# Queries and keys of a two-layer encoder made by rows of 512 columns and turned by VectorE and DRAM, in place of products by channels

## The chip, the cores and the metric

The kernel runs on one core of one Trainium2 chip, as one launch. The metric is the device time of the launch in microseconds (us), the median of the runs; smaller is better. Profiles are of one execution each, taken by the hardware profiler.

## What is computed

Two layers, each with a token mixer and a gated MLP, on 256 tokens of 1024 channels, all in float32. The mixer, cut to what matters here:

```python
u, q, k, v, g_pool, g_attn = split(rmsnorm(h) @ w_in)     # 1024, 1536, 1536, 1536, 1024, 1024 columns
pool_out = per_group(centred_mean(u) - u) @ w_pool * pool_scale
logits = q @ k.T * HEAD_DIM**-0.5 + bias                  # 12 heads of 128 channels, 3 groups of 4 heads
p = softmax over a head of all three groups together      # keys +-64 strides of 1, 4, 16 tokens
attn = p @ v
merged = sigmoid(g_pool) * (pool_out @ w_a) + sigmoid(g_attn) * (attn @ w_b)
h = h + merged @ w_o
```

The MLP (`w_up`, a convolution over three tokens, gelu, `w_down`) follows, and a last norm after the second layer.

## The kernel before

**Products.** A float32 weight is loaded raw (1 MB a load, on SP's queue), and cut into *pieces* of 128 x 1024 elements. ScalarE rounds a piece to the high part `wh` (L201), VectorE subtracts to get the low part `wl` (L203); this is called the split. The activation is kept as two parts too, and a product is three matmuls: high by high, high by low, low by high. Raw loads have 3 buffers, split pieces 5 (`RAW`, `BUFS`, L104), and `W.get()` (L224) asks for splits of up to three pieces ahead (`LOOK`). All splits go through ScalarE and VectorE in the order of the program's list of pieces.

There are two ways to form a product with the normed activation `x2`. *By channels* (`proj` L551, `two_sums` L530): a piece is 128 output channels; for each of 8 parts of the depth one matmul of `wh` against 512 columns (both parts of 256 tokens) and one of `wl` against 256, 16 matmuls a piece; the result has channels on partitions. *By tokens* (`by_tokens` L672, `v_sum` L661): the tokens are on the output's partitions, a piece is 256 rows of depth by 512 output columns, 12 matmuls of 512 columns; four pieces make 512 columns, in two PSUM tiles, one for each half of the tokens.

**Order in a layer.** Values (by tokens), the pooling branch's `u` (by channels), then queries and keys: `PAIRS` (L38) lists six pairs of heads, and for each, two pieces of queries and two of keys go through `proj` (L1115 to L1147). Then `po2 @ w_a` (`pa`, two blocks by tokens, L1151), the first gate (two blocks, L1163), the second gate with `attn @ w_b` (L1177), `w_o`, and the MLP. The w_pool product (`pool_out`, L993) is dealt out over the second pair.

**Queries and keys.** Four heads (group 0) are kept in two parts, `qh`, `kh` and `qkl` (ScalarE L1131, VectorE L1132 and L1136); the other eight are kept as plain float32 `q`, `kk` (ScalarE L1142, VectorE L1143). The factor HEAD_DIM^-0.5 is put on the queries here.

**Attention.** `scores(hh)` (L1025) makes, for each half of the tokens, a PSUM tile `s_ps`: three matmuls of the high and low parts (L1029), and a float32 one for each of the other groups (L1034, two records each). VectorE adds the bias (L1040) and takes the maximum (L1045), ScalarE the exponential (L1048), VectorE the reciprocal of the sum (L1050) and the scaling (L1051). `start_turn` hands the two tiles to `cross` (L704): VectorE transposes 32 x 32 blocks (L711), SP writes them to DRAM (L713), waits, and reads them back with 4 DMAs in another order (L718), which completes a transposition. `turn` splits part of it (L1072, L1073), `weigh` (L1076) multiplies by the values into `o_ps`, and ScalarE and VectorE keep that as `at2` (L1091, L1092). The MLP uses the same `cross` for its gate.

**What sets the order.** The table `steps` (L1095) says after which piece of the stages from the fourth pair on each of these is written into the program; `step()` runs it. From the program a scheduler makes one fixed list of instructions for each engine. An engine works through its list in order, so an instruction that waits holds up what is behind it. SP's list holds the loads and the crossings together; `loads_behind` puts named loads behind named reads.

Of the kernel before, what the change touches and what calls it, by code (L numbers as in the profile page):

```python
# [16 lines left out]
P = 128  # L17
D = 1024
# [19 lines left out]
PAIRS = (2, 4, 0, 1, 3, 5)  # L38
# [58 lines left out]
class Weights:  # L97
# [8 lines left out]
    def __init__(self, tc, pool, idle):  # L106
        self.tc, self.nc, self.pool, self.idle = tc, tc.nc, pool, idle
        self.loads, self.pieces = [], []
        self.n_loaded, self.n_split, self.n_got = 0, 0, 0
        self.raw, self.split = {}, {}  # L110
        self.live = set()
        self.behind, self.later = (), []
        self.last = [None, None]
        self.loads_behind = {}
# [12 lines left out]
    def load(self, upto):  # L127
        while self.n_loaded < min(upto, len(self.loads)):
            src, shape, tag = self.loads[self.n_loaded]
            name = f"raw{self.n_loaded}"  # L130
            if tag is None:
                t = self.pool.tile([P, *shape], F32, tag="raw", bufs=self.RAW, name=name)
            else:
                t = self.idle.tile([P, *shape], F32, tag=tag, name=name)
            held = self.loads_behind.get(self.n_loaded)
            with self.tc.issue_after(held.ins) if held else ExitStack():
                self.last_load = self.nc.sync.dma_start(out=t, in_=src)
            self.raw[self.n_loaded] = t
            self.n_loaded += 1

# [101 lines left out]
def encoder(ctx, tc, x, w_in, w_pool, pool_scale, w_a, w_b, w_o, norm1, norm2, w_up, conv_w,  # L242
# [28 lines left out]

    first_up = []
    for l in range(DEPTH):
# [10 lines left out]
        for n, c in enumerate(PAIRS):  # L284
            pool = ([], [])
            if n == 1:
                pool = W.add(
                    w_pool[l].rearrange("g (k p) c -> p (g k) c", p=P), (8, 256),
                    [((lambda t, j=j: t[:, 4 * j : 4 * j + 4, :]), (4, 256)) for j in range(2)],
                )  # L290
                pool = (pool[:1], pool[1:])
            W.use(pool[0] + cols(w_in[l], C_Q + c * 256))
            W.use(pool[1] + cols(w_in[l], C_K + c * 256))
# [378 lines left out]
    def by_tokens(x2, n, at_once=1, then=None, ps=None, begin=0, end=None):  # L672
# [4 lines left out]
        for i0 in range(begin, n if end is None else end, at_once):  # L677
            held = [W.get() for _ in range(at_once)]
# [25 lines left out]
    def cross(rows, y, z, name, but=1, after=None):  # L704
# [4 lines left out]
        with tc.issue_after(after.ins) if after else ExitStack():  # L709
# [3 lines left out]
        nc.sync.dma_start(  # L713
            out=d.rearrange("(t p) q x -> p t (q x)", t=2),
            in_=y.rearrange("p t q c j -> p t (q c j)"),
        )
# [5 lines left out]
        W.loads_behind[W.n_loaded + but] = there  # L722
# [180 lines left out]
    for l in range(DEPTH):  # L903
# [114 lines left out]
        qh = big.tile([P, HPG, 2, P], F32R, tag="q0", name="qh")  # L1018
        kh = big.tile([P, HPG, 2, P], F32R, tag="k0", name="kh")
        q = big.tile([P, NH - HPG, 2, P], F32, tag="q1", name="q")  # L1020
        kk = big.tile([P, NH - HPG, 2, P], F32, tag="k1", name="k")
        at2 = big.tile([P, HPG, 2, 2, P], F32R, tag="at2", name="at2")
        probs, ptiles = {}, {}

        def scores(hh):  # L1025
            for t in range(2):
                ps = acc.tile([P, 512], F32, tag="acc", name="s_ps")
                for m, (a, b) in enumerate(((qh, kh), (qh, kl), (ql, kh))):
                    nc.tensor.matmul(  # L1029
                        ps[:, 0:256], a[:, hh, t, :], b[:, hh].rearrange("p t m -> p (t m)"),  # L1030
                        start=(m == 0), stop=(m == 2),
                    )
                for g in (1, 2):
                    nc.tensor.matmul(  # L1034
                        ps[:, 128 + g * 128 : 256 + g * 128], q[:, (g - 1) * HPG + hh, t, :],
                        kk[:, (g - 1) * HPG + hh, t, :],
                        start=True, stop=True,
                    )
                s = sm.tile([P, 512], F32, tag="s", name="s")
                nc.vector.tensor_add(  # L1040
                    out=s.rearrange("p (a b) -> p a b", a=2), in0=ps.rearrange("p (a b) -> p a b", a=2),
                    in1=bias_of(t, hh),
# [15 lines left out]
        turned_p = big.tile([P, 2, 2 * 4, 4, 32], F32, tag="ybig", name="turned_p")  # L1058

        def start_turn(hh):  # L1060
            y = sm.tile([P, 2, 4, 4, 32], F32, tag="gain", bufs=1, name="turning")
            there = cross([probs[hh, t] for t in range(2)], y, turned_p[:, hh % 2], "turning")
# [3 lines left out]
        def turn(hh):  # L1066

            z = turned_p[:, hh % 2]
# [7 lines left out]
        def weigh(hh):  # L1076
# [31 lines left out]
        places = iter(range(20))  # L1108
# [5 lines left out]

        for m, c in enumerate(PAIRS):  # L1115
            if m == 1:
                po2 = two_parts("m2", "po2")
                pool_parts = pool_out(po2)
            if m == 2:

                qkl = big.tile([P, 2, HPG, 2, P], F32R, tag="xn", name="qkl")
                ql, kl = qkl[:, 0], qkl[:, 1]
            for n in range(4):
                if m == 1:
                    next(pool_parts)
                src, rest = (halves(a) for a in proj(x2, 1 + (m != 1)))
                hd = 2 * c + n % 2
                scale = HD**-0.5 if n < 2 else 1.0
                if hd < HPG:
                    hi, lo = ((qh, ql) if n < 2 else (kh, kl))  # L1130
                    nc.scalar.mul(out=hi[:, hd], in_=src, mul=scale)  # L1131
                    nc.vector.scalar_tensor_tensor(  # L1132
                        out=lo[:, hd], in0=src, scalar=scale, in1=hi[:, hd].bitcast(F32),
                        op0=ALU.mult, op1=ALU.subtract,
                    )
                    nc.vector.scalar_tensor_tensor(  # L1136
                        out=lo[:, hd], in0=rest, scalar=scale, in1=lo[:, hd].bitcast(F32),
                        op0=ALU.mult, op1=ALU.add,
                    )
                else:  # L1140
                    o = (q if n < 2 else kk)[:, hd - HPG]
                    nc.scalar.mul(out=o, in_=rest, mul=scale)  # L1142
                    nc.vector.scalar_tensor_tensor(  # L1143
                        out=o, in0=src, scalar=scale, in1=o, op0=ALU.mult, op1=ALU.add
                    )
                if m >= 3 and n % 2:
                    step()  # L1147


        pa = big.tile([P, 2, D], F32, tag="xn", name="pa")  # L1150
        for cc in HALVES:  # L1151
            ps = by_tokens(po2, 4, then=step)
            for t in range(2):
                nc.scalar.copy(out=pa[:, t, cc], in_=ps[t])

        def gate():
            ps = by_tokens(x2, 4, then=step if steps else None)
            th = big.tile([P, 2, 512], F32, tag="gates", name="gates")
# [4 lines left out]
        for cc in HALVES:  # L1163
# [211 lines left out]
```

## Time and profile before

| | |
|---|---|
| median of 3 runs | 859.91 us (859.57 to 860.25) |
| the profiled execution | 859.81 us, of which the profile's span is 858.0 us |
| VectorE busy | 661.2 us, 77% of the span |
| ScalarE busy | 493.8 us, 58% |
| GpSimd busy | 32.0 us, 4% |
| DMA | 186.81 MB, 217 GB/s over the span, 63.8% of 16 engines' time |

PE is TensorE, DVE VectorE, ACT ScalarE, POOL GpSimd, SP SyncE (its queue issues nearly all DMAs). Busy time is the union of an engine's instructions. In groups, "x24 | 5.7, 708" means 24 instructions, 5.7 us busy in all, 708 ns for one; matmuls overlap in the pipeline, so their own duration is longer than the time from one start to the next.

### The profile page before, as it was taken

How to read it: one execution, taken by the hardware profiler on the slowest of the kernel's cores; microseconds unless marked ns; L12 is line 12 of the kernel's file. 1: busy time of each engine (PE TensorE's matmuls, PEld its weight loads, DVE VectorE, ACT ScalarE, POOL GpSimd, SP SyncE). 2: the span in 40 equal slices, each digit the busy share in tenths (PEclk: the TensorE clock that was granted, in tenths of full speed). 3: DMA queues.
4: the chain of work that ended last, by engine and by line, in shares of the span. 5: the costliest groups of instructions: out<-in, count | busy, mean ns of one | idle time of the engine just before them, and what ended most of it. 6: DMA issues, size and time to landing. Idle time of an engine off the chain costs nothing.

```text
span 858.0 us, 11823 instructions
## 1 busy us (share of the span) xinstructions
PE 851.6 (99%) x4343; PEld 727.9 (85%) x4343; DVE 661.2 (77%) x1050; ACT 493.8 (58%) x795; POOL 32.0 (4%) x98
## 2 busy tenths in 40 slices
PE   9999999999999999999999999999999999999997
PEld 8888888888888888888888889988888888888886
DVE  7998796667767788888855987874776777988894
ACT  7756654455445476666645665543654555775672
POOL 1710000000010000000000000000000000000001
PEclk9999999999999999999999999999999999999999
DMA  9686547766747876666736555658667478676641
GB/s 331 217 248 206 196 163 231 240 228 229 250 182 246 270 249 231 231 235 206 245 99 209 184 199 192 198 175 268 226 243 275 154 249 259 246 256 208 239 147 49
DMA packets 136387, 186.81 MB, mean 218 GB/s; under 512 B 5561, under 2 KB 88193, under 8 KB 136329
## 3 DMA queue, kind: packets, MB, share of 16 engines
q1 hardware_dynamic: 136168, 185.79, 63.8%
q8 instruction: 34, 0.56, 0.3%
q10 hardware_dynamic: 160, 0.27, 0.1%
q14 instruction: 25, 0.20, 0.1%
HBM read 172.39 MB, written 13.65 MB: 217 GB/s over the span
## 4 chain that ended last, share of the span: by engine, by line
PE 99%; DVE 0%; ACT 0%; POOL 0%; issue 0%; POOLq 0%; ACTq 0%
PE proj_ps L543 34%; PE t_ps L667 30%; PE v_ps L667 6%; PE res_ps L586 6%; PE res_ps L585 6%; PE res_ps L587 6%; PE v_ps L895 3%; PE v_ps L802 1%; PE pool_ps L543 1%; PE o_ps L1086 1%; PE s_ps L1034 1%; PE s_ps L1029 1%; PE o_ps L1082 1%; PE xt_ps L481 1%; PE gain_ps L372 0%; PE xt_ps L750 0%
## 5 line engine op out<-in xcount | busy, mean ns | idle before, releaser
L203 DVE TENSOR_TENSOR wl<-raw,wh 128x1024 fp32r<-128x1024 f32 x274 | 329.8, 1217 | 88.1 <-ACT wh L201 73.6
L201 ACT CAST wh<-raw 128x1024 fp32r<-128x1024 f32 x274 | 284.3, 1049 | 118.3 <-PE t_ps L667 49.0
L543 PE MATMUL proj_ps<-x,wh 128*128 128x512 f32 x832 | 196.9, 390 | 0.0
L543 PEld LDWEIGHTS proj_ps<-x,wh 128*128 128x128 f32 x832 | 154.3, 188 | 30.9
L667 PE MATMUL t_ps<-wh,x 128*128 128x512 f32 x576 | 179.7, 390 | 0.0
L667 PEld LDWEIGHTS t_ps<-wh,x 128*128 128x128 f32 x576 | 107.8, 188 | 22.3
L667 PE MATMUL t_ps<-wl,x 128*128 128x512 f32 x288 | 112.1, 389 | 0.0
L543 PEld LDWEIGHTS proj_ps<-x,wl 128*128 128x128 f32 x832 | 105.4, 191 | 3.0
L543 PE MATMUL proj_ps<-x,wl 128*128 128x256 f32 x832 | 107.8, 283 | 0.0
L586 PE MATMUL res_ps<-wl,actq 128*128 128x512 f32 (+1 forms) x184 | 70.0, 380 | 0.0
L587 PE MATMUL res_ps<-wh,actk 128*128 128x512 f32 (+1 forms) x184 | 69.9, 380 | 0.0
L585 PE MATMUL res_ps<-wh,actq 128*128 128x512 f32 (+1 forms) x184 | 69.7, 381 | 0.0
L667 PEld LDWEIGHTS t_ps<-wl,x 128*128 128x128 f32 x288 | 54.1, 188 | 11.2
L667 PE MATMUL t_ps<-wh,po 128*128 128x512 f32 x128 | 41.4, 395 | 0.0
L587 PEld LDWEIGHTS res_ps<-wh,actk 128*128 128x128 f32 x184 | 34.6, 188 | 6.6
L586 PEld LDWEIGHTS res_ps<-wl,actq 128*128 128x128 f32 x184 | 34.6, 188 | 6.4
L585 PEld LDWEIGHTS res_ps<-wh,actq 128*128 128x128 f32 x184 | 34.5, 188 | 6.3
L454 POOL TENSOR_SCALAR ss<-ss 128x1 f32<-128x1 f32 x8 | 2.0, 253 | 779.6 <-ACT junk L447 779.6
L1308 ACT CAST actq<-g 128x256 fp32r<-128x256 f32 x44 | 17.0, 403 | 20.7 <-DVE g L1297 20.0
L667 PEld LDWEIGHTS t_ps<-wh,po 128*128 128x128 f32 x128 | 24.0, 188 | 4.9
L447 ACT ACTIVATE junk<-h 128x512 f32<-128x512 f32 (+1 forms) x19 | 10.5, 553 | 28.6 <-DVE h L445 28.5
L579 ACT COPY a<-proj_ps 128x256 f32<-128x256 f32 x36 | 13.6, 389 | 23.3 <-PE proj_ps L543 23.3
(204 smaller groups left out, 1148.9 us busy)
## 6 DMA issues: line engine op xcount, KB each, us to landing
raw<-in_w_in_dram SPq DMA_DIRECT2D x58, 1024.0 KB, 5.4
raw<-in_w_up_dram SPq DMA_DIRECT2D x44, 1024.0 KB, 6.9
raw<-in_w_down_dram SPq DMA_DIRECT2D x22, 1024.0 KB, 4.7
raw<-in_w_a_dram SPq DMA_DIRECT2D x8, 1024.0 KB
raw<-in_w_o_dram SPq DMA_DIRECT2D x8, 1024.0 KB, 7.1
crossing<-crossing SPq DMA_DIRECT2D x12, 512.0 KB, 5.4
turning<-turning SPq DMA_DIRECT2D x8, 512.0 KB, 2.8
turned_p<-turning SPq DMA_DIRECT2D x32, 128.0 KB, 3.3
```

What stands on the lines that cost most here:

```text
L201: inst = nc.scalar.copy(out=h, in_=src)
L203: inst = nc.vector.tensor_sub(out=l, in0=src, in1=h.bitcast(F32))
L447: nc.scalar.activation(junk[:, 0 : cc.stop - cc.start], h[:, t, cc], AF.Square, scale=D**-0.5, accum_out=ss[:, n : n + 1],)
L481: nc.tensor.transpose(pt[:, k, :], xn[:, c0 : c0 + P], ident)
L543: nc.tensor.matmul(out, w(k), x, start=(steps is first and k == 0), stop=(steps is last and k == nk - 1), skip_group_check=turns["rest"],)
L579: nc.scalar.copy(out=out, in_=sums[1])
L585: nc.tensor.matmul(ps, ah, wh, start=first, stop=False, skip_group_check=on)
L586: nc.tensor.matmul(ps, ah, wl, start=False, stop=False, skip_group_check=on)
L587: nc.tensor.matmul(ps, al, wh, start=False, stop=last, skip_group_check=on)
L667: nc.tensor.matmul(ps, x2[:, 2 * n + j, part, t, :], w[:, j, :], start=(n + m == 0), stop=(n == last and m == 5),)
L895: nc.tensor.matmul(ps[t], a[:, k, t, :], w[:, j, :], start=(k + m == 0), stop=(k == KD - 1 and m == 2),)
L1308: nc.scalar.copy(out=ah, in_=g)
```

## The change

Six pieces of 256 columns' queries and keys give way to three *blocks* of four heads' queries and keys, each made by tokens, 512 columns at a time, and turned to channels by `cross`. Queries and keys of block 0 are the four heads of group 0, of block 1 heads 0 and 1 of the other groups, of block 2 their heads 2 and 3.

- A load of these weights is 512 rows by two times 256 columns, in two DMAs of 0.5 MB, where it was one DMA of 1 MB. The number of pieces and of splits stays the same.
- The six products (`n` 0 to 5) are each followed by `cross`, 12 in all in the two layers: two transposes, a write of 0.5 MB, four reads of 128 KB. `cross` now also keeps its write behind the reads of the crossing before.
- Group 0 is cut into its parts from the crossed tiles (`parts`: ScalarE and VectorE, two instructions of 128 x 512 each for queries and for keys). Keys of the other groups are used as they land; queries are copied by ScalarE (`bring`, 128 x 1024). VectorE and ScalarE no longer combine the two sums of every head.
- The factor HEAD_DIM^-0.5 goes into the addition of the bias.
- `pool_out` is dealt out over the second product.
- `steps` has 40 places in place of 20, one after each piece of these blocks, `pa` and the first gate. Scores of the four heads stand behind places 21, 25, 29, 33 (pieces 41, 45, 50, 54 of the layer's list), `weigh` behind 29, 33, 37, 39. The first MLP load is written at place 39.
- `pa`, the gates, the lows and the turned rows move to other buffers.

```diff
-PAIRS = (2, 4, 0, 1, 3, 5)
+BLOCKS = ((0, 1), (2, 4), (3, 5))
...
+            for columns, some in src if isinstance(src, list) else ((slice(None), src),):
+                self.last_load = self.nc.sync.dma_start(out=t[:, :, columns], in_=some)
...
     def cross(rows, y, z, name, but=1, after=None):
...
-        nc.sync.dma_start(
-            out=d.rearrange("(t p) q x -> p t (q x)", t=2),
-            in_=y.rearrange("p t q c j -> p t (q c j)"),
-        )
+        with tc.issue_after(W.there.ins) if W.there else ExitStack():
+            nc.sync.dma_start(
+                out=d.rearrange("(t p) q x -> p t (q x)", t=2),
+                in_=y.rearrange("p t q c j -> p t (q c j)"),
+            )
...
-                nc.vector.tensor_add(
+                nc.vector.scalar_tensor_tensor(
                     out=s.rearrange("p (a b) -> p a b", a=2), in0=ps.rearrange("p (a b) -> p a b", a=2),
-                    in1=bias_of(t, hh),
+                    scalar=HD**-0.5, in1=bias_of(t, hh), op0=ALU.mult, op1=ALU.add,
                 )
...
+        def parts(which):
+
+            hi = (qh, kh)[which]
+            for half in range(2):
+                a = kk[:, 1 - which, :, 2 * half : 2 * half + 2].rearrange("p a c j -> p c a j")
...
+                with W.after_splits():
+                    nc.scalar.copy(out=h_, in_=a)
+                    nc.vector.tensor_sub(out=l_, in0=a, in1=h_.bitcast(F32))
+
+        def bring(half):
+
+            a = tmp[:, 0].rearrange("p (a c j) -> p c a j", a=8, c=4)
+            with W.after_splits():
+                nc.scalar.copy(out=q[:, half].rearrange("p c t (a j) -> p c (t a) j", j=32), in_=a)
...
         steps = {
-            0: ((scores, 0), (start_turn, 0)),
-            2: ((scores, 1), (start_turn, 1)),
-            3: ((turn, 0),),
-            4: ((weigh, 0),),
-            6: ((turn, 1), (scores, 2), (start_turn, 2)),
-            7: ((weigh, 1),),
-            8: ((scores, 3), (start_turn, 3)),
-            12: ((turn, 2),),
-            13: ((weigh, 2),),
-            14: ((turn, 3),),
-            15: ((weigh, 3),),
+            8: ((parts, 0),),
+            12: ((parts, 1),),
+            16: ((bring, 0),),
+            21: ((scores, 0), (start_turn, 0)),
+            24: ((bring, 1),),
+            25: ((scores, 1), (start_turn, 1)),
+            28: ((turn, 0),),
+            29: ((weigh, 0), (scores, 2), (start_turn, 2)),
+            32: ((turn, 1),),
+            33: ((weigh, 1), (scores, 3), (start_turn, 3)),
+            36: ((turn, 2),),
+            37: ((weigh, 2),),
+            38: ((turn, 3),),
+
+            39: ((weigh, 3), (W.load_one, first_up[l][1])),
         }
...
-        for m, c in enumerate(PAIRS):
...
-                src, rest = (halves(a) for a in proj(x2, 1 + (m != 1)))
...
+        for n in range(6):
+            block, which = divmod(n, 2)
+            if n == 1:
+                po2 = two_parts("m2", "po2")
+            ps = by_tokens(x2, 4, then=step, ahead=pool_out(po2) if n == 1 else None)
+            y = tmp[:, 1].rearrange("p (t q c j) -> p t q c j", t=2, q=4, c=4)
+            if n in (2, 4):
+                z = tmp[:, 0].rearrange("p (a c j) -> p a c j", a=8, c=4)
+            else:
+
+                z = kk[:, (1, 0, None, 0, None, 1)[n]]
+            cross(ps, y, z, "crossing", int(n == 0), W.last[1])
...
+        for n in range(2):
             ps = by_tokens(po2, 4, then=step)
+            pa.append(big.tile([P, 2, 512], F32, tag=("q0", "k0")[n], name="pa"))
             for t in range(2):
-                nc.scalar.copy(out=pa[:, t, cc], in_=ps[t])
+                nc.scalar.copy(out=pa[n][:, t], in_=ps[t])
```

**The lists as built.** The scheduler does not keep to the places of `steps`. Below is what the changed kernel's lists hold at three places of the first layer; the second layer has the same with other piece numbers. Pieces 38 to 45 are the last block's queries and keys, 46 to 53 `w_a`, 54 to 61 the first gate, 62 to 65 and 66, 67 half of the second gate and of `w_b`. Lines are those of the changed kernel.

```
TensorE   piece 45 | s_ps of heads 0 and 1, their L1060 products (4 tiles) | piece 46: wh, wh, wl ...
ScalarE   wh45 | exp (head 0, tile 0) | wh46 | exp (head 0, tile 1) | wh47
VectorE   wl45 | bias, bias (head 0) | max, max | 1/z | bias (head 1) | scaling | wl46 | 1/z | transpose | scaling | wl47

TensorE   piece 49 | piece 50: wh, wh, wl ...
ScalarE   wh49 | exp, exp (head 1) | pa (tile 0 of pieces 46-49) | bring | pa (tile 1) | wh50 | wh51
VectorE   wl49 | max | bias | max | 1/z | scaling | 1/z | scaling | wl50 | transpose, transpose | wl51

TensorE   piece 51..53 | o_ps of head 0 and L1054 of head 2 within 53 | L1060 of head 2 (2 tiles) | piece 54: wh, wh, wl ...
ScalarE   wh53 | turn | at2 (head 0) | exp (head 2, tile 0) | wh54 | exp | wh55
VectorE   wl53 | turn | at2 (head 0) | bias | max | bias | max | 1/z | scaling | wl54 | 1/z | transpose | scaling | wl55
```

The L1054 products of heads 0 and 1 stand between pieces 41 and 42; their L1060 products stand behind piece 45. Scores of head 3 stand within piece 57, `o_ps` of heads 2 and 3 within pieces 61 and 65.

More of the change, by code (lines that the diff above doesn't have):

```diff
@@ L128, in load, with load_one @@
         while self.n_loaded < min(upto, len(self.loads)):
[L129 to L138, printed above, removed]
-            self.n_loaded += 1
+            if self.n_loaded not in self.raw:
+                self.load_one(self.n_loaded)
+            self.n_loaded += 1
+    def load_one(self, n):
+        src, shape, tag = self.loads[n]
+        if tag is None:
+            t = self.pool.tile([P, *shape], F32, tag="raw", bufs=self.RAW, name=f"raw{n}")
+        else:
+            t = self.idle.tile([P, *shape], F32, tag=tag, name=f"raw{n}")
+        held = self.loads_behind.get(n)
+        with self.tc.issue_after(held.ins) if held else ExitStack():
+            for columns, some in src if isinstance(src, list) else ((slice(None), src),):
+                self.last_load = self.nc.sync.dma_start(out=t[:, :, columns], in_=some)
+        self.raw[n] = t
     def load_by(self, n):
@@ L1054, in scores @@
                 probs[hh, t] = p
-        turned_p = big.tile([P, 2, 2 * 4, 4, 32], F32, tag="ybig", name="turned_p")
         def start_turn(hh):
             y = sm.tile([P, 2, 4, 4, 32], F32, tag="gain", bufs=1, name="turning")
-            there = cross([probs[hh, t] for t in range(2)], y, turned_p[:, hh % 2], "turning")
+            turned[hh] = turned_p[:, hh % 2]
+            there = cross([probs[hh, t] for t in range(2)], y, turned[hh], "turning")
             if hh == HPG - 1:
@@ L1188, in encoder @@
                     )
[L1189 to L1190 removed]
+                    nc.vector.tensor_add(out=th[:, t], in0=th[:, t], in1=pa[n][:, t])
+                turning, there, made = to_chunks(
                     th[:, t], y[:, t], z[:, t], (mh[:, ks, t], ml[:, ks, t])
```

142 lines of the change are left out of this document (70 added, 72 removed).

## Prediction

> **What bounds the kernel now.** I read the page's busy times first, then the chain of work that ended last, in order of time.
>
> ```profile
> span 858.0 us, 11823 instructions
> ...
> PE 851.6 (99%) x4343; PEld 727.9 (85%) x4343; DVE 661.2 (77%) x1050; ACT 493.8 (58%) x795; POOL 32.0 (4%) x98
> ```
>
> TensorE is busy 99% of the span. So 1 us off TensorE's list is 1 us off the time, and 1 us in which TensorE waits is 1 us on it. Everything else costs only through such a wait. The chain stays on TensorE until the last norm, and gives its rates without the overlap of the pipeline (start, us, what, records):
>
> ```profile
> 0.76 2.90 PE gain_ps L372 x12
> ...
> 108.56 0.44 PE s_ps L1034 x4
> 109.00 11.11 PE proj_ps L543 x64
> ...
> 133.53 0.89 PE o_ps L1086 x8
> ...
> 259.23 38.08 PE t_ps L667 x168
> ```
>
> By channels, 64 matmuls are four pieces, 512 columns' worth: 11.11 us. By tokens, one matmul takes 38.08/168 = 0.2267 us, and the same 512 columns take 48 of them: 10.88 us. A tile's L1034 products (four records) take 0.44 us.
>
> **The sum, part 1: TensorE's own work.** In two layers 12 blocks of 512 columns go from 11.11 to 10.88 us: 12 x 0.23 = **2.8 us less**. The products for pooling, scores and values keep number and shape; that the float32 score products now read keys in blocks of 32 is no news, since L1086 reads its tile so and takes the same 0.11 us a record (0.89/8) as L1034 (0.44/4). That is all that the change can win, since the rest of its work is not on TensorE.
>
> **Part 2: work beside TensorE.** Groups, shapes kept apart, durations in ns before the last bar:
>
> ```profile
> L203 DVE TENSOR_TENSOR wl<-raw,wh 128x1024 fp32r<-128x1024 f32 x274 | 329.8, 1217 | 88.1 <-ACT wh L201 73.6 <-PE proj_ps L543 13.7
> L201 ACT CAST wh<-raw 128x1024 fp32r<-128x1024 f32 x274 | 284.3, 1049 | 118.3 <-PE t_ps L667 49.0 <-PE res_ps L587 18.4 <-PE proj_ps L543 12.0
> ...
> L1143 DVE SCALAR_TENSOR_TENSOR k<-proj_ps,k 128x256 f32<-128x256 f32 x16 | 6.6, 414 | 3.3 <-ACT k L1142 3.3
> ...
> L1154 ACT COPY pa<-t_ps 128x512 f32<-128x512 f32 x8 | 4.7, 586 | 15.9 <-PE t_ps L667 15.8
> ...
> L1091 ACT CAST at<-o_ps 128x256 fp32r<-128x256 f32 x8 | 2.9, 365 | 15.7 <-PE o_ps L1086 15.7
> ```
>
> VectorE loses 64 combinations, at L1143's 0.414 us (32 for plain heads, two for each of 16 in parts), 26.5 us, and gains 24 transposes of 0.65 (L711 below, 1.30 for two) and 8 subtractions, half the elements of L203, 0.6: 20.4 us. ScalarE loses 48 copies of 128 x 256, at L1091's 0.365 17.5 us, and gains 8 of 128 x 512 (`parts`, as L1154) of 0.59 and 4 (`bring`, the elements of L201) of 1.05: 9 us. `bring` reads in strides; at twice its time it would put 1 us more on piece 50 below. The bias addition with a factor keeps its old time, as it reads and writes the same. As busy time all this lies under TensorE and costs nothing.
>
> Over the second product the two by-tokens tiles hold two of four PSUM slots while pooling turns over the other two, where it had three. A slot comes free after a ScalarE and a VectorE instruction of 0.5 us, and a piece of 2.7 us lies between: 0, with 1 us a layer as the other end.
>
> **DMA.** 12 crossings move 1 MB each (0.5 out, 0.5 back) besides the loads. The MLP already does this at the same pace:
>
> ```profile
> core 0: us, PE busy (x) PEld busy (x) DVE busy (x) ACT busy (x) POOL busy (x), PEclk, DMA share, GB/s
> 88.00:107.00 19.00, 19.00 (x111) 16.77 (x110) 13.43 (x24) 11.28 (x18) 0.00 (x0) 1.00 0.58 192
> 259.00:297.00 38.00, 38.00 (x169) 31.45 (x169) 29.53 (x46) 21.24 (x34) 0.00 (x0) 1.00 0.82 268
> 852.00:855.00 3.00, 0.31 (x3) 0.11 (x1) 0.91 (x2) 1.53 (x5) 0.95 (x3) 1.00 0.01 4
> 855.00:858.00 3.00, 0.00 (x0) 0.00 (x0) 0.00 (x0) 0.00 (x0) 0.00 (x0) 0.51 0.46 175
> ```
>
> From 259 to 297 us there is a crossing and two loads in every 11 us, at 0.82 of the DMA engines, and TensorE is busy 38.00 of 38. Queries and keys went at 0.58 without crossings; with them I take 0.8 to 0.9. Behind a crossing's write SP waits, and the loads wait behind it:
>
> ```profile
> 281.77 0.37 SPq L713 DMA_DIRECT2D crossing<-crossing  x1
> 287.61 1.81 SPq L718 DMA_DIRECT2D zg<-crossing  x4
> ```
>
> ```profile
> DMA to landing us min/median/max: 2.3/2.5/7.1
> ```
>
> That is the longest of the four there. From the write's issue to the last read's, 7.7 us pass, and with a landing (of all the crossing's DMAs) of 2.5 to 7.1 us the data is there after 10 to 15 us. `parts` and `bring` hold up a split that TensorE wants eight pieces, 22 us, after the block's end; transposes ahead and copies behind take some 3 us. So loads and crossings cost **0**, with 4 us or more to spare; if that cover were gone, TensorE would pay what is late, us for us. Halving each load's DMA adds 24 issues of about 0.4 us to SP, which stands waiting in these stretches, and the `norm2` gain and the first MLP load, put later in SP's list, are wanted only after `w_o`: 0 too.
>
> **Part 3: the lists.** Here the change costs. A split that stands in ScalarE's or VectorE's list behind an instruction that waits for a TensorE result can't be made before that result. I counted in the built lists how many matmuls lie between such a result and the first use of the next split behind it. Before, after the first ten microseconds, the smallest count is 14 (3.2 us): an `at` copy, a cast and a subtraction take 0.37 + 1.05 + 1.22 = 2.6 us, and so nothing waits. After, in each layer, it is 5 at piece 46, 1 at piece 50, 3 at piece 54, 13 at 58, 10 at 62, 5 at 66. The scores now stand against the piece that they hold up. How fast such a chain runs is in the timeline at head 0 and (143 us) head 2:
>
> ```profile
> 109.01 1.28 DVE L1040 TENSOR_TENSOR s<-s_ps,bt 128x512 f32<-128x512 f32 x2
> 110.21 1.27 DVE L1045 TENSOR_REDUCE nm<-s 128x1 f32<-128x512 f32 x2
> 111.39 1.21 DVE L203 TENSOR_TENSOR wl<-raw,wh 128x1024 fp32r<-128x1024 f32 x1
> 112.52 0.21 DVE L1050 RECIPROCAL rz<-z 128x1 f32<-128x1 f32 x2
> 112.71 0.88 DVE L1051 TENSOR_SCALAR p<-p,rz 128x512 f32<-128x512 f32 x2
> 113.51 1.30 DVE L711 STREAM_TRANSPOSE turning<-p 128x512 f32<-128x512 f32 x2
> ...
> 143.54 0.69 DVE L1040 TENSOR_TENSOR s<-s_ps,bt 128x512 f32<-128x512 f32 x1 [1.75 <-PE s_ps L1034]
> ```
>
> ```profile
> 110.91 0.73 ACT L1048 ACTIVATE p<-s,nm 128x512 f32<-128x512 f32 x1 [3.10 <-DVE nm L1045]
> 111.54 0.19 ACT L1048 ACTIVATION_READ_ACCUMULATOR p<-s,nm 128x1 f32 x1
> 111.64 0.71 ACT L1048 ACTIVATE p<-s,nm 128x512 f32<-128x512 f32 x1
> ...
> 144.99 0.72 ACT L1048 ACTIVATE p<-s,nm 128x512 f32<-128x512 f32 x1 [1.20 <-DVE nm L1045]
> ```
>
> The exponential starts 1.90 us after the first bias addition when two additions go first, 1.45 us when one does; the next on ScalarE starts 0.73 later.
>
> *Piece 46.* Count from TensorE's start on the last products of heads 0 and 1 (4 tiles, 4 x 0.44 = 1.78 us). First tile 0.45; exponential 2.35; `wh46` from 3.08 to 4.13. VectorE has the sum at 3.2; 1/z, bias of head 1, scaling (0.1 + 0.65 + 0.45) end at 4.4; `wl46` (1.2, with what its waits add) ends at 5.6 at the latest, 5.4 at the earliest, 5.5. TensorE can do two matmuls with `wh46` (0.45): it stands 5.5 - 1.78 - 0.45 = **3.3 us**.
>
> *Piece 54* (two tiles, 0.89): 0.45; exponential 1.9; `wh54` 2.63 to 3.68; `wl54` 4.9: 4.9 - 0.89 - 0.45 = **3.55 us**.
>
> *Piece 50.* `wh50` stands behind both `pa` copies, the second of which needs the end of piece 49. After that end: copy 0.59, cast 1.05, subtraction 1.22, and 0.1 to 0.3 for the `bring` between the copies, less 0.1 of overlap a step: 2.9. Less 0.45: **2.5 us**.
>
> *Pieces 58 to 66.* At 58, 13 matmuls (two of them the slower score products) give 2.4 us for bias, `at`, maximum and split, 2.85: 0.45. At 59 the chain waits twice for ScalarE (two `pa` copies, then the exponential): about 1.1. At 62, 2.3 us against 2.6: 0.3. At 66, 1.1 against 2.6: 1.5. Together **3.35 us**; bounds 0 and 5.
>
> A layer: 3.3 + 3.55 + 2.5 + 3.35 = 12.7 us; two layers 25.4. The profiled execution took 859.81 us (858.0 of span and 1.8 around it), 0.1 below the median of the runs, so: 859.8 - 2.8 + 25.4 = **882.4 us**. With the small ones at 0 and the big ones at two thirds it is 859.8 - 2.8 + 2 x 6.2 = 869.4; with the small ones at 5 and half a microsecond more at each big one, 859.8 - 2.8 + 2 x 15.85 = 888.7.
>
> **Rivals.**
>
> *The waits are covered (faster).* One mechanism: TensorE reaches the score products with splits to spare, as before, where `wl` leads by at least 14 matmuls; then only part 1 is left, 857.0 us. It decides at piece 46: this holds if `wl46` is done before TensorE leaves the score products. For it: VectorE and ScalarE have less to do and reach the scores early. Against it: their lists are fixed, and the exponential ahead of `wh46` can't start before TensorE's product. I give it 0.05, and 0.03 to a remainder that nearly eats the 2.8 us (859 to 861).
>
> *The clock falls in the pauses.* TensorE's last matmuls end near 852.3 us; the granted clock is still 1.00 to 855 and then 0.51, so it falls after some 2.7 us of standing still, or a little more. The launch's first 12 records of 128 columns take 2.90 us where 0.11 each would be 1.3: 1.6 us, the price of a cold start, though the clock column shows no dip for it. If each of the six long pauses paid that, it is 882.4 + 9.6 = 892. Against it: each pause is broken by two matmuls, and the longest unbroken stand is 2.8 us (piece 54, from 0.89 to 3.68). The chance is 0.09. The Trainium skill, "TensorE: Matmul & The Clock Gate", section "Why this matters for your kernels", asks for no idle gap over about 3 us between bursts, or the clock goes back to half; by that rule piece 54 stands at the edge, and the tail of the trace agrees with such a bound.
>
> *DMA is what is late.* From piece 42 to 53 four round trips through DRAM (two crossings, two turned heads) share SP's queue with six loads in about 35 us. If every step took as long as the slowest above (6 us from a write to its reads, 1.8 to issue them, 7 to land), the keys of head 2 would land some 3 us after TensorE wants them: 882.4 + 6 = 888. For it: SP's list alternates write, load, reads. Against it: the pauses at 46 and 50 give it 6 us. The chance is 0.07.
>
> **How the numbers follow.** The forecast, 869 to 889 with 882.4 as the likeliest, has 0.76, and the rivals the other 0.24. The range, 868 to 892, takes in the forecast with its bounds, the late DMA and the clock's case up to its price, and leaves out the two covered cases. A difference of 0.2% (1.7 us) is about what a measurement of this kernel can tell from none: faster 0.05, within 0.03, slower 0.92.
>
> **What would show it.** The counts: 448 `proj_ps` matmuls of 512 columns where there were 832. TensorE idle time of about 25 us in the groups of `t_ps`, released by ScalarE's `wh` and VectorE's `wl` at pieces 46, 50, 54, with TensorE busy near 849. VectorE idle ahead of the bias addition, released by `s_ps`. No TensorE wait for a DMA in queries and keys, DMA share there 0.8 to 0.9. I would be wrong if TensorE's idle time is under 10 us, or if it lies in the blocks of queries and keys.

## The result and the profile after

The changed kernel takes 895.34 us (median of 4 runs, 894.19 to 896.31), the kernel before 860.08 us (859.57 to 860.27): a ratio of 1.041, 95% interval 1.0392 to 1.0428. The profiled execution took 895.75 us, 35.9 more than that of before. The page, its first lines and four of its groups:

```profile
span 893.9 us, 11515 instructions
...
PE 862.6 (97%) x4151; PEld 721.4 (81%) x4151; DVE 658.7 (74%) x1018; ACT 483.9 (54%) x759; POOL 31.0 (3%) x98
...
L688 PE MATMUL t_ps<-wl,x 128*128 128x512 f32 x480 | 189.7, 395 | 3.5 <-DVE wl L208 3.5
L564 PE MATMUL proj_ps<-x,wh 128*128 128x512 f32 x448 | 106.5, 390 | 0.0
...
L688 PE MATMUL t_ps<-wh,po 128*128 128x512 f32 x128 | 42.7, 408 | 8.2 <-ACT wh L206 8.2
...
L1065 DVE SCALAR_TENSOR_TENSOR s<-s_ps,bt 128x512 f32<-128x512 f32 x16 | 10.8, 685 | 41.5 <-PE s_ps L1060 41.5
```

TensorE stands still for 893.9 - 862.6 = 31.3 us, where it was 6.4: 24.9 us more. Of its idle time 22.8 us lie ahead of `t_ps` products, released by `wh` and `wl` (two of these groups are above), and VectorE waits 41.5 us for the score products: the places are those that were expected. But TensorE's *busy* time also grew, from 851.6 to 862.6, although it has fewer matmuls. Its timeline at pieces 46, 50 and 54 (start, us, what; in brackets the idle time ahead):

```profile
136.12 1.95 PE L1060 MATMUL s_ps<-k,q 128*128 128x128 f32 x16
140.48 0.73 PE L688 MATMUL t_ps<-wh,po 128*128 128x512 f32 x2 [2.42 <-ACT wh L206]
141.88 0.80 PE L688 MATMUL t_ps<-wl,po 128*128 128x512 f32 x1 [0.66 <-DVE wl L208]
142.47 1.06 PE L688 MATMUL t_ps<-wh,po 128*128 128x512 f32 x2
143.32 0.63 PE L688 MATMUL t_ps<-wl,po 128*128 128x512 f32 x1
143.75 0.63 PE L688 MATMUL t_ps<-wh,po 128*128 128x512 f32 x1
...
153.65 0.39 PE L688 MATMUL t_ps<-wh,po 128*128 128x512 f32 x1
155.74 0.73 PE L688 MATMUL t_ps<-wh,po 128*128 128x512 f32 x2 [1.69 <-ACT wh L206]
156.99 0.50 PE L688 MATMUL t_ps<-wl,po 128*128 128x512 f32 x1 [0.52 <-DVE wl L208]
...
169.92 1.05 PE L1060 MATMUL s_ps<-k,q 128*128 128x128 f32 x8
173.81 0.73 PE L688 MATMUL t_ps<-wh,x 128*128 128x512 f32 x2 [2.84 <-ACT wh L206]
175.07 0.50 PE L688 MATMUL t_ps<-wl,x 128*128 128x512 f32 x1 [0.53 <-DVE wl L208]
```

A pause is best measured from start to start. At 46: sixteen records of 0.11 and two matmuls of 0.227 should bring `wl46` at 136.12 + 1.78 + 0.45 = 138.35; it starts at 141.88, **3.5 us** late (3.3 were expected). In the same way 50 costs 156.99 - 154.33 = **2.7** (2.5) and 54 costs 175.07 - 171.26 = **3.8** (3.55). The three chains of the prediction run as it wrote them down. What it did not have is behind the pause at 46: the matmuls of 143.32 and 143.75 are 0.43 us apart, nearly twice 0.227. The windows of 2 us there (second column TensorE's busy time, `PEclk` the third from the end):

```profile
138.00:140.00 2.00, 0.07 (x1) 0.00 (x0) 1.71 (x5) 1.32 (x3) 0.00 (x0) 1.00 0.00 0
140.00:142.00 2.00, 0.85 (x3) 0.42 (x3) 2.00 (x5) 2.00 (x5) 0.00 (x0) 0.89 0.00 0
142.00:144.00 2.00, 2.00 (x5) 1.63 (x6) 2.00 (x4) 1.98 (x3) 0.00 (x0) 0.50 0.00 0
144.00:146.00 2.00, 2.00 (x8) 1.56 (x8) 2.00 (x4) 0.00 (x0) 0.00 (x0) 0.75 0.22 87
146.00:148.00 2.00, 2.00 (x11) 1.64 (x10) 2.00 (x4) 0.00 (x0) 0.00 (x0) 1.00 0.93 255
```

The granted clock is at half for 3.4 us (a *dip* from here on), and from its first matmul there TensorE counts as busy: the row from 142 has 5 matmuls in 2 us, the one at full clock from 146 has 11. Of the four dips in the execution two lie behind piece 46 and two behind 54. All excess of TensorE's start times over the full-clock rates, both layers together:

| place | expected, us | measured, us |
|---|---|---|
| pause at 46 | 6.6 | 7.1 |
| pause at 50 | 5.0 | 5.3 |
| pause at 54 | 7.1 | 7.6 |
| pauses at 58 to 66 | 6.7 | 9.1 |
| half clock behind 46 and 54 | 0 (9.6 as a rival) | 6.5 |
| wait ahead of the second norm | 0 | 1.7 |
| start of the program | 0 | 1.0 |
| rest: TensorE's own work | -2.8 | -2.4 |
| sum | 22.6 | 35.9 |

### The profile page after: what moved, and what is told of

Same layout as the page of the kernel before. It is cut to its first block, busy times and chain, and to the rows that moved or that the text cites. A ratio compares the mean times of both kernels' runs of the same rounds, so it can differ in the third digit from the quotient of the medians.

```text
span 893.9 us, 11515 instructions
## 1 busy us (share of the span) xinstructions
PE 862.6 (97%) x4151; PEld 721.4 (81%) x4151; DVE 658.7 (74%) x1018; ACT 483.9 (54%) x759; POOL 31.0 (3%) x98
## 4 chain that ended last, share of the span: by engine, by line
PE 89%; DVE 4%; ACT 3%; DMA 2%; issue 1%; SPq 0%; POOL 0%; POOLq 0%; ACTq 0%; DVEq 0%
PE t_ps L688 40%; PE proj_ps L564 17%; PE v_ps L688 6%; PE res_ps L608 6%; PE res_ps L607 6%; PE res_ps L606 6%; PE v_ps L921 2%; DVE wl L208 2%; PE pool_ps L564 1%; PE v_ps L828 1%; ACT wh L206 1%; DMA turned_p<-turning 1%; PE o_ps L1110 1%; DMA turning<-turning 1%; PE o_ps L1106 1%
## 5 line engine op out<-in xcount | busy, mean ns | idle before, releaser
L688 PE MATMUL t_ps<-wh,x 128*128 128x512 f32 x960 | 303.2, 393 | 5.7 <-ACT wh L206 5.7
L688 PEld LDWEIGHTS t_ps<-wh,x 128*128 128x128 f32 x960 | 180.9, 189 | 44.2 <-ACT wh L206 6.5
L688 PE MATMUL t_ps<-wl,x 128*128 128x512 f32 x480 | 189.7, 395 | 3.5 <-DVE wl L208 3.5
L688 PEld LDWEIGHTS t_ps<-wl,x 128*128 128x128 f32 x480 | 91.0, 190 | 25.5 <-DVE wl L208 6.7
L564 PE MATMUL proj_ps<-x,wh 128*128 128x512 f32 x448 | 106.5, 390 | 0.0
L564 PEld LDWEIGHTS proj_ps<-x,wh 128*128 128x128 f32 x448 | 83.1, 188 | 16.6
L564 PEld LDWEIGHTS proj_ps<-x,wl 128*128 128x128 f32 x448 | 56.9, 191 | 1.9
L564 PE MATMUL proj_ps<-x,wl 128*128 128x256 f32 x448 | 57.5, 283 | 0.0
L1065 DVE SCALAR_TENSOR_TENSOR s<-s_ps,bt 128x512 f32<-128x512 f32 x16 | 10.8, 685 | 41.5 <-PE s_ps L1060 41.5
L1073 ACT ACTIVATE p<-s,nm 128x512 f32<-128x512 f32 x16 | 11.6, 725 | 50.6 <-DVE nm L1070 49.6
```

The source lines that it names most:

```text
L564: nc.tensor.matmul(out, w(k), x, start=(steps is first and k == 0), stop=(steps is last and k == nk - 1), skip_group_check=turns["rest"],)
L688: nc.tensor.matmul(ps, x2[:, 2 * n + j, part, t, :], w[:, j, :], start=(n + m == 0), stop=(n == last and m == 5),)
L1065: nc.vector.scalar_tensor_tensor(out=s.rearrange("p (a b) -> p a b", a=2), in0=ps.rearrange("p (a b) -> p a b", a=2), scalar=HD**-0.5, in1 ...
L1073: nc.scalar.activation(p, s, AF.Exp, bias=nm[:, 0:1], accum_out=z)
```

## The experiments

Theory of the lists: the splits of pieces 46 to 66 stand in ScalarE's and VectorE's lists behind instructions that wait for TensorE, so TensorE pauses, and the pauses also cost clock. Rivals: it is the data that is late (crossings, SP's queue); the matmuls behind a pause are slow for another reason than the clock; a pause that is taken away comes back at the next place.

**scores_behind.** The bias additions, and with them all behind them, are put behind the splits that are already asked for:

```diff
+                with W.after_splits():
                     nc.vector.scalar_tensor_tensor(   # the bias addition of scores(hh)
```

> The changed kernel with one thing undone: the bias additions of the scores stand behind the splits already asked for on VectorE and ScalarE; work and data stay the same. Smallest counts of matmuls in the built lists: pieces 46, 54 and 58 go from 5, 3 and 13 to 15 or more, piece 50 stays at 1, piece 66 at 4, piece 62 goes from 10 to 13. Theory of the lists: the pauses at 46 and 54 go with the slow clock behind them, and those at 58 and 59; the one at 50 stays at 2.6 us, 66 stays. 895.3 - 2 x (3.5 + 1.7 + 3.8 + 1.5 + 1.5) - 1.0 = about 870 us. Rival, late data (crossings and SP's queue): the splits come early, but TensorE then waits for the scores' data or the chain behind it waits for a DMA: 885 or more, with TensorE's idle time released by a DMA.

Measured: 875.93 us, 1.0186 of before (1.0171 to 1.0201). The pauses at 46 and 54 and their dips are gone, 19.4 us, with no other work and no other data: these two were the order of the lists. But 870 us were expected. The profiled execution took 878.01, 8 more than that, and its trace shows some 5 of them: a start 1.2 us slower than in the changed kernel's trace, small waits between 51 and 56 (1.0 and 1.6 us in the two layers), and a dip at 50 in the first layer alone. The rest, and what the other three executions (875.62 to 876.09 us) lost, is open.

The slow start is the clock too, by the pace of the products there. The same three products in this run, and then in the changed kernel:

```profile
7.99 1.63 PE L828 MATMUL v_ps<-m,xuh 128*128 128x512 f32 x3
...
7.66 0.95 PE L828 MATMUL v_ps<-m,xuh 128*128 128x512 f32 x3
```

From 8.56 to 9.84 us they start 0.43 us apart here, the rate of a dip, and 0.23 apart from there on; the clock column has 1.00 for all of it, so at the start it does not show this.

The dip at 50 tells something, since the pause is the same in both layers (the first layer, the second, and then the clock in both):

```profile
151.75 0.73 PE L688 MATMUL t_ps<-wh,po 128*128 128x512 f32 x2 [1.62 <-ACT wh L206]
153.01 0.64 PE L688 MATMUL t_ps<-wl,po 128*128 128x512 f32 x1 [0.53 <-DVE wl L208]
```

```profile
582.77 0.73 PE L688 MATMUL t_ps<-wh,po 128*128 128x512 f32 x2 [1.62 <-ACT wh L206]
584.03 0.50 PE L688 MATMUL t_ps<-wl,po 128*128 128x512 f32 x1 [0.52 <-DVE wl L208]
```

```profile
153.00:155.00 2.00, 1.99 (x5) 1.60 (x6) 2.00 (x4) 0.00 (x0) 0.00 (x0) 0.56 0.57 218
155.00:157.00 2.00, 2.00 (x6) 1.52 (x6) 1.87 (x5) 1.88 (x5) 0.00 (x0) 0.59 0.51 149
...
584.00:586.00 2.00, 1.97 (x9) 1.62 (x10) 2.00 (x4) 0.14 (x1) 0.00 (x0) 1.00 0.67 242
```

**busy_pause.** The last score product of head 1 is repeated sixteen times:

```diff
-                for g in (1, 2):
+                for g in (1, 2) + (2,) * AGAIN.get((hh, t), 0):   # AGAIN = {(1, 1): 16}
```

> The changed kernel, with the last score product of head 1 (128 columns) repeated 16 times into the same place; the result stays the same. The lists of VectorE, ScalarE and SP are the same; on TensorE 12 repeats (1.3 us) stand in the pause ahead of wh46 and 4 (0.45 us) in the one ahead of wl46. Piece 54 is left as it is, as a control. Theory of the clock: the pause at 46 keeps its end, but TensorE no longer stands still for 2.4 us at a stretch, and the matmuls after it run at 0.227 us at once; 1.5 to 1.7 us a layer less: 892 us, granted clock 1.00 at 140 to 148 us and still 0.6 to 0.7 behind piece 54. Rival: the slow matmuls after the pause come from the weights' arrival or the restart of the piece and not from the clock: 895 us and slow matmuls as before.

Measured: 894.56 us (1.0403 of before, 1.0387 to 1.0418), where 892 was expected: inconclusive by its time, clear by its trace. (Each product is two records of 0.11, so the repeats fill 2.7 us of the pause and not 1.3.) The time from the score products to `wl46` is 5.76 us as before, the matmuls behind run at full speed, and at piece 54 the dip is still there. But now piece 50 has one, where the changed kernel had none, at the same pause of 1.69 and 0.53 us:

```profile
140.00:142.00 2.00, 2.00 (x14) 1.81 (x13) 2.00 (x5) 2.00 (x5) 0.00 (x0) 1.00 0.00 0
142.00:144.00 2.00, 2.00 (x11) 1.64 (x10) 2.00 (x3) 0.95 (x2) 0.00 (x0) 1.00 0.00 0
...
152.00:154.00 2.00, 0.73 (x2) 0.30 (x2) 0.76 (x1) 2.00 (x3) 0.00 (x0) 1.00 0.36 136
154.00:156.00 2.00, 1.48 (x4) 1.20 (x5) 2.00 (x4) 2.00 (x4) 0.00 (x0) 0.50 0.09 27
156.00:158.00 2.00, 2.00 (x7) 1.61 (x6) 2.00 (x3) 0.57 (x2) 0.00 (x0) 0.65 0.90 252
```

So the matmuls behind a pause are slow where the clock is at half and only there, and it is not the length of a pause alone that decides.

**pooling_behind.** Only the copies to `pa` are put behind the splits:

```diff
+            with W.after_splits():
                 for t in range(2):
                     nc.scalar.copy(out=pa[n][:, t], in_=ps[t])
```

> The changed kernel with the two copies of the pooled product to pa put behind the splits already asked for, and nothing else. The count at piece 50 goes from 1 to over 14 matmuls; the others stay. Theory of the lists: the pause at 50 (2.66 us a layer) goes, those at 46 and 54 stay: 895.3 - 5.3 = 890 us. Rival, each pause only moves the next one: what is won at 50 is lost at 54, and the time stays at 894 to 896.

Measured: 889.11 us (1.0336, 1.0321 to 1.0352), 6.2 less than the changed kernel, of which the profiles put 1.1 to a faster start (the changed kernel's trace has a wait of 0.9 us for the load of `h` there). The pause at 50 is gone in both layers, those at 46 (2.41 and 0.66 us of idle time) and 54 (2.84 and 0.53) stand as they were. This pause does not move on to the next place, so the sum of the prediction's third part may be taken piece by piece here.

**pauses_filled.** All three pauses are filled with products that nobody reads, at 46 with the repeats of busy_pause:

```diff
+            if n == 0:                          # behind piece 49, ahead of the copies to pa
+                fill(FILL[0], last_mm[0])       # FILL = (14, 16); 128 columns each, a PSUM tile of their own
...
+            if hh == 2:
+                fill(FILL[1], made_ps[2])
```

> The changed kernel with products of 128 columns that nobody reads put into all three long pauses: 16 repeats at piece 46 as in busy_pause, 14 (1.55 us) ahead of piece 50, 16 (1.8 us) ahead of piece 54. The lists of VectorE, ScalarE and SP are those of the changed kernel, and so the pauses keep their ends. Theory of the clock, as busy_pause and the changed kernel left it (a dip lasts 3.4 us at half clock, costs 1.6 us, and follows a stretch of 3.4 us in which TensorE worked half the time or less): no dip is left, granted clock 0.998, and four times 1.6 us are saved: 889 us. Rival: something other than the clock slows the matmuls behind a pause: 894 to 896 us.

Measured: 890.41 us (1.0353, 1.0339 to 1.0367), 4.9 less, although TensorE is busy for 875.6 us there, 13 more. The four dips are gone. The repeats at 50 outlast the pause by 0.5 us a layer, and one new dip came up at piece 66 of the second layer. With these 2.6 us the four dips come to 7.5 us, of which the profiles put 0.8 to a faster start: 6.7, near the 6.5 of the table, 1.6 to 1.7 us a dip. With the pauses' ends kept and more work on TensorE the time falls: it is the clock, and not something else behind a pause, that costs these 6.5 us.

**lists_mended.** Scores, `pa` and the `at` copies, all behind the splits:

```diff
+            with W.after_splits():          # in weigh; for the last head written only behind pieces 66 and 67
                 nc.scalar.copy(out=oh, in_=ps)
                 nc.vector.tensor_sub(out=ol, in0=ps, in1=oh.bitcast(F32))
```

> The changed kernel with the scores, the copies to pa and the at copies all behind the splits already asked for (the at copies of the last head behind pieces 66 and 67 too). Every count is 15 or more. Theory of the lists: all pauses at 46 to 66 and both dips of the clock go, 2 x 18 us; what is left is the gain of TensorE's own work, 2.8 us, less a wait of 0.85 us a layer ahead of the second norm: 857 to 860 us, beside 860.1 of the kernel before. Rival, late data: without the pauses the crossings and the turned heads come too late, and TensorE waits for DMAs at pieces 46 to 66: 864 us or more.

Measured: 868.67 us (1.0097, 1.008 to 1.0113). 26.7 us are back, but 857 to 860 were expected, and here the rival is right in part. With the pauses gone, the next wait is one for a DMA. ScalarE at piece 54, and SP's list ahead of it:

```profile
162.00 1.04 ACT L206 CAST wh<-raw 128x1024 fp32r<-128x1024 f32 x1 [7.01 <-DMA raw<-in_w_in_dram]
```

```profile
148.61 0.40 SPq L739 DMA_DIRECT2D crossing<-qk_rows  x1
154.19 1.78 SPq L744 DMA_DIRECT2D k<-crossing  x4
156.08 0.39 SPq L143 DMA_DIRECT2D raw<-in_w_in_dram  x1
```

The last crossing is written at 148.61; SP waits 5.6 us until it may be read, and the load of pieces 54 and 55 is held behind these reads. It lands at 162. TensorE loses 3.5 us from piece 54 to 57 in the first layer and 2.6 in the second. At piece 54 itself it is 1.6 and 0.9; the rest comes behind it, at piece 56 with `wh56` behind the exponentials of head 2 in ScalarE's list, so it is order again.

**lists_only** and **load_ahead.** The first moves the gates' tanh behind the splits and head 2's scores back by two pieces, and leaves SP's list alone; the second also lets that load go ahead of the last crossing's reads:

```diff
-            cross(ps, y, z, "crossing", int(n == 0), W.last[1])
+            cross(ps, y, z, "crossing", int(n in (0, 5)), W.last[1])
```

> lists_mended with two places more: the scores of head 2 asked for two pieces later, and the tanh of the gates behind the splits already asked for; SP's list as in the changed kernel, where the load of pieces 54 and 55 is held behind the reads of the last crossing. Every count is 18 or more. Theory: what is left at 54 is a wait for that load (raw issued at 156.1 us, there at 162.0), so the waits at 54 to 56 (3.5 us a layer) stay, and only piece 66 gains, 1 to 1.6 us a layer: 866 us. Rival: the wait at 54 was one of the lists after all: 859 us.

> lists_only with one thing more: the load of pieces 54 and 55 may go ahead of the last crossing's reads on SP, right behind its write. Theory of late data in SP's queue: the load lands 6 to 7 us earlier, TensorE waits for no DMA, and 7 us go: 859 us, with the wait of 0.85 us a layer ahead of the second norm left. Rival: the DMA engines are what is short, and the reads of the crossing, now behind the load, come late instead: 863 to 866 us, with waits for the keys of head 2.

Measured: lists_only 864.12 us (1.0047, 1.0034 to 1.0061) and load_ahead 862.38 us (1.0028, 1.0016 to 1.0039). The load is worth less than was thought, 1.7 us and not 7, since lists_only had already brought back most of the waits at 54 to 57: 0.9 and 0.6 us a layer are left there, with ScalarE still waiting for the load until 160.93 us. Its two list changes are not told apart, and the load was also issued 1.3 us earlier in its trace. What is left with the load ahead is, from start to start, 0.7 to 0.9 us each at pieces 56, 57 and 59 of the first layer and at 59 of the second.

**all_mended.** Also the split between the two residual additions goes behind the second:

```diff
+            if t == 0 and m == 1:     # the piece held back until here, its split behind this addition
+                W.later = W.later[-3:] + [((norm.added,), range(piece + 2, piece + 3))]
```

> load_ahead with the split of the piece that stands between the two residual additions of the first token half on VectorE put behind the second of them, as it stands in the kernel before. Theory: the wait ahead of the second norm (0.85 us a layer) goes, and what is left is the change's gain on TensorE, 2.8 us, up to the difference of the start (0.6 to 2 us from run to run): 857 to 858 us. Rival: that wait is not from this order, or the split is late instead: 859 us or more.

Measured: 861.80 us (1.0019, 1.001 to 1.0028), where 857 to 858 were expected. The wait ahead of the second norm falls from 0.8 to 0.2 us a layer in the traces; the medians differ by 0.6 us, which their intervals cannot tell from none. Waits of 0.7 us each are left at pieces 57 and 59 of both layers. Behind the first stands in the chain the load of pieces 56 and 57, and the DMA share (second to last column) of the windows around it shows why it is late:

```profile
156.79 9.00 DMA raw<-in_w_in_dram
```

```profile
136.00:148.00 12.00, 12.00 (x59) 10.04 (x59) 12.00 (x20) 4.49 (x8) 0.00 (x0) 1.00 0.42 141
148.00:160.00 12.00, 12.00 (x61) 10.21 (x60) 7.01 (x12) 6.32 (x12) 0.00 (x0) 1.00 0.92 297
160.00:172.00 12.00, 11.26 (x55) 8.94 (x55) 7.38 (x12) 4.83 (x8) 0.00 (x0) 1.00 0.98 295
```

From 136 to 148 us VectorE works without a break (12.00 of 12) and SP waits for its transposes; the DMA engines stand at 0.42, and then, from 143 to 157 us, SP issues the writes of two turned heads and a crossing, the reads of the first head and of the crossing, and three loads. The last of these takes 9.0 us to land.

**keys_first.** SP's list in another order:

```diff
-            21: ((scores, 0), (start_turn, 0)),
-            24: ((bring, 1),),
+            21: ((scores, 0),),
+            24: ((start_turn, 0), (bring, 1)),
...
-            29: ((weigh, 0),),
-            31: ((scores, 2), (start_turn, 2)),
+            31: ((weigh, 0), (scores, 2), (start_turn, 2)),
```

> all_mended with SP's list near the scores in another order: head 0 is turned after the last crossing instead of ahead of it, so that the loads of pieces 52 to 55 go ahead of its write; the products of head 0 with the values are asked for two pieces later. Every count is 15 or more. In all_mended TensorE still waits 1.7 to 2.2 us a layer at pieces 56 to 58, and the chain leads from there to a load that took 9.0 us to land, while the DMA share was 0.92 to 0.98. Theory of SP's order: DMA stands at 0.42 from 136 to 148 us because SP waits for VectorE there; with loads moved into that gap the waits at 56 to 58 go: 857 to 859 us. Rival: too much data is moved between 136 and 172 us, whatever the order, and some load or some head's data is late: 861 us or more.

Measured: 861.71 us (1.0017, 1.0004 to 1.003); the profiled execution has a span of 858.5 us. In it TensorE waits nowhere in the scores any more, and the load is spread out:

```profile
136.00:148.00 12.00, 12.00 (x62) 10.16 (x62) 11.65 (x19) 6.01 (x9) 0.00 (x0) 1.00 0.82 270
148.00:160.00 12.00, 12.00 (x55) 9.93 (x54) 9.53 (x14) 5.57 (x9) 0.00 (x0) 1.00 0.75 228
160.00:172.00 12.00, 12.00 (x67) 10.25 (x66) 6.04 (x11) 4.40 (x8) 0.00 (x0) 1.00 0.88 290
```

The waits at 56 to 59 came from the order of SP's list and of the steps, then, and not from too much data. Yet the time is that of all_mended, the rival's number and not the 857 to 859 expected, and a little above before: with the waits of the changed kernel taken out, the change gains nothing. From the first pooling product to the first of `w_b` the trace of before takes 128.64 us (73.84 to 202.48) and this one 128.06 (74.23 to 202.29), 0.6 us less, where five blocks should save 1.15; from there to the first product of `w_down` it takes 0.9 and 0.4 us more in the two layers. These are gaps of about 0.1 us at changes from one kind of product to another; I did not take them apart. The start differs too, without a pattern that follows the code: the last of the first 24 products of `v_ps`, the group shown for scores_behind, starts at 12.18 to 14.66 us in the eleven traces, at 12.43 in that of before. The latest is scores_behind's. No version here beats the kernel before.

## Why the prediction was wrong

**Right.** Direction, place and mechanism: slower, by splits behind waiting instructions at 46, 50, 54 and 58 to 66. scores_behind and pooling_behind show it by order alone. The three long pauses fit to 0.3 us each. That idle time was put at 25.4 us and the profile has 24.9 more is in part luck: from start to start the pauses cost 29.1 us, and the idle time counts less of each but takes in 2.0 us at the norm and the start. The waits of queries and keys for DMA did not come; TensorE works there in the changed kernel without a break, at a DMA share of 0.70 to 0.78 where 0.8 to 0.9 were expected:

```profile
64.00:88.00 24.00, 24.00 (x115) 20.15 (x114) 20.34 (x34) 15.32 (x24) 0.00 (x0) 1.00 0.78 253
88.00:112.00 24.00, 24.00 (x108) 19.87 (x107) 17.22 (x22) 13.60 (x19) 0.00 (x0) 1.00 0.70 233
```

The cover for DMA of "4 us or more" held too, but by the time that the pauses gave; lists_mended shows what is missing without them, 0.9 to 1.6 us a layer at piece 54 and up to 3.5 with what follows from it. The rival of late data was set aside with just this argument, that the pauses give it time.

**The step that failed is the rival "the clock falls in the pauses".** It had the right price, 1.6 us (measured 1.55 to 1.7), in part by luck, since that was read from twelve records at the start that run at half pace for 2.9 us, and a dip lasts 3.4. But it had a chance of 0.09 and no place in the sum, for one reason: "the longest unbroken stand is 2.8 us", against a delay of "some 2.7 us of standing still" read from the tail of the trace. That delay was a coincidence: in the eleven traces the clock falls 2.0 (lists_mended) to 5.3 us (lists_only) after the last matmul. The dips of these runs begin at fixed marks, not at a fixed time after work ends. In the changed kernel they begin at 141.58, 175.70, 581.90 and 616.02 us (from windows of 1 us; the clock is either full or half, so a mean of 0.79 from 141 to 142 is half clock for 0.42 us): 10, 119 and 10 times 3.413 us apart. What goes with them is TensorE's busy share in the 3.41 us stretch ahead of a mark:

| kernel | dips begin at, us | busy share of the stretch before |
|---|---|---|
| the change | 141.6, 175.7, 581.9, 616.0 | 21%, 40%, 21%, 39% |
| busy_pause | 154.0, 174.5, 594.3, 614.8 | 50%, 37%, 48%, 39% |
| pooling_behind | 141.3, 172.0, 578.2, 608.9 | 39%, 44%, 21%, 24% |
| scores_behind | 153.2 | 37% |
| pauses_filled | 654.7 | 50% |

(Shares by the modelled ends of the matmuls.) All 14 dips follow stretches with 21 to 50% of work. Of the stretches with 53 to 80%, 23 in the same runs away from the start and the end of the program, none is followed by one. Within the programs no stretch breaks this; at an end one does: in lists_only the stretch from 854.1 to 857.5 us has 46%, and the clock stays full up to 860.9. So the share is the rule of these traces and not known to be what the chip counts. Two stands of 1.6 and 0.5 us can therefore cost a dip or not, as they fall into one stretch or across a mark: that is why piece 50 dips in the first layer of scores_behind and not in the second, where the stretch had 53%.

**The range failed with it.** Its top, 892, took the upper bound of the pauses (888.7) and the clock's case (892.0, made with pauses of middle size) as cases beside each other. They are not: the clock falls *in* the pauses, and so its price comes on top of theirs. Pauses at their upper bound with six dips give 859.8 - 2.8 + 31.7 + 9.6 = 898; the measured 895.3 lies within. The clock is the largest miss, but not the only one that it took: without its 6.5 us the time would be 888.8, and without the 5.1 us of the smaller terms below and the start 890.2, both inside the range.

**Smaller terms.** The pauses at 58 to 66 were put at 3.35 us a layer and took 4.55 (66 alone 2.1 for 1.5). The wait ahead of the second norm, 0.85 us a layer, was not in the sum; it comes from a VectorE list in which a split stands between two residual additions, and all_mended takes it out by order alone. The gain of TensorE's own work, 2.8 us, is 2.4 as the rest of the table, a remainder, and as good as nothing in the versions without pauses: in keys_first 0.6 us a layer up to `w_b` where 1.15 were expected, and 0.9 and 0.4 lost behind it.

## What to carry to other kernels

Count, for each instruction that waits for a product, how many matmuls lie between that product and the first use of what stands behind it in the same list; when that is less than the chain takes, the difference is TensorE's, and it can be summed piece by piece. Add the clock to such pauses, not beside them, as soon as a few of them in 3.4 us leave TensorE half idle. And when a wait is taken out, look for the one that it covered: here a load in SP's queue stood behind three pauses, and behind it there was no gain left.

## What the runs showed of the hardware

In these traces the clock is decided in stretches of 3.41 us, on marks that do not start with the program: the first dips of the changed kernel (141.6 us) and of busy_pause (154.0) lie 3.6 stretches apart, though their lists are the same up to the repeats. Within the programs each stretch with 21 to 50% of work is followed by one at half clock, 3.41 us long in all 14 cases. The Trainium skill, "TensorE: Matmul & The Clock Gate", section "What's actually happening", has a free-running window of 3413 ns and has the clock fall after an idle window. The length and the marks agree with these traces. That the window has to be idle does not: one with 50% of work was enough, with stands of 1.2 and 0.5 us in it (pauses_filled, 654.7 us).
